# A two-layer encoder trunk with its residual stream turned: features on partitions instead of tokens, and the RMS taken by a product with ones

## The chip, the cores and the metric

One core of a Trainium2 chip runs the whole program in one launch. The metric is the device time of that launch in microseconds. Three runs of the kernel before were timed, and one more execution was taken with the hardware profiler.

## What is computed

There are 512 tokens of 1024 features, and two layers. Each layer is a mixer with a gate, a residual add, and a gated per-layer embedding (PLE). The reference, cut to what matters here:

```python
def rmsnorm(x, g):
    y = x * rsqrt(mean(x * x, axis=-1) + EPS)
    return y * g

for i in range(2):
    xn = rmsnorm(x, norm_g[i])
    if i == 0:                      # neighbourhood attention, 16 heads of 64
        q, k, v, z = split(xn @ na_w_in)
        y = (na(q, k, v, rpb) * silu(z)) @ na_w_out
    else:                           # latent attention, 16 heads
        c_q, c_kv, k_rope, z = split(xn @ mla_w_in)
        y = (mla(c_q, c_kv, k_rope) * silu(z)) @ mla_w_out
    h = x + y
    gate = sigmoid(rmsnorm(h, ple_norm[i]) @ ple_w_gate[i])
    x = h + gate * (p[i] @ ple_w_proj[i])
return rmsnorm(x, final_norm)
```

All matrices are float32.

## The kernel before

**Products.** Each operand is split into a high and a low part of the matmul type fp32r, and a product is three matmuls for each 128 rows of its contraction: high by high, low by high, high by low. A tile over 1024 features is 24 matmuls of 128 x 128 by 128 x 512. `load_w` (L67 to L78) brings weights: a DMA into `wraw`, a copy to `whi` on ACT (L76), and the rest `wlo = wraw - whi` on POOL (L77). Weight buffers rotate: three in the common pool, and more in a pool of the stage (`extra=True`).

**Layouts.** The attention parts already work with features on partitions: their input `xT` is the normalised x with 128 features on the partitions and 512 tokens along the row, split into `xh` and `xl`. The residual stream is the other way: four tiles of 128 tokens by 1024 features (`x`, later `r`). So every normalisation is in rows. `rms` (L100 to L107) squares a tile on ACT with a sum along the row, takes (mean + eps) to the power -0.5 of that one column on POOL (L106), and multiplies on DVE by it and by the gain (L107). After it `rows_to_cols` turns the tile with eight TensorE transposes (L118), and `split` makes the high and low parts (L83 on ACT, L85 on DVE). This is done for x (tiles named `xn`), for h in both layers (`hn`), and for the x between the layers (`x1n`).

**Stages, in order.**

- Start: x is loaded, normalised and turned; PLE's product p @ w_proj (`ple`) runs on TensorE meanwhile and is written to DRAM.
- `z_phase` makes five of the eight gate tiles of layer 0; then the 16 heads, and the last three gate tiles.
- `out_proj` (L345): for each half n of the 1024 output features and each of four token tiles t, 24 matmuls with the attention output as stationary operand and the weights (512 columns) moving. A tile is added to `r` (L357). When n is 1, tile t is complete, and `norm_h` normalises and turns it into `hnT[t]`.
- `gate_phase` (L383): the same loops over n and t with `hnT[t]` stationary; sigmoid on ACT (L398), times the PLE tile (L399), added to `r` (L401). In layer 0 a complete tile is stored to `spill`, normalised and turned into `x1T`. In layer 1 `done` scales each tile with the final norm and sends it out (L636 to L649); the last tile is cut into two halves of 256 columns.
- Layer 1: `mla_c` makes the compressed q and kv and the rotary key with tokens on partitions (`c`), normalises them there and turns them (`cn`); then seven gate tiles, the heads, PLE of layer 1 and again `out_proj` and `gate_phase`.

**Order.** The order on each engine is made when the program is built: a scheduler that simulates a timeline places each instruction, and every engine then runs its own list strictly in that order, each instruction waiting for what it needs. PSUM tiles rotate by tag: two for `mm`, two for `S`, three for `T`, one for `O`.

Of the kernel before, what the change touches and what calls it, by code (L numbers as in the profile page):

```python
# [19 lines left out]
P = 128  # L20
S = 512
# [17 lines left out]
class Trunk:  # L39
    def __init__(self, tc, ctx, a, dbg=None):  # L40
# [10 lines left out]
        self.half = self.const.tile([P, 1], F32, name="half")  # L51
        nc.vector.memset(self.half, -0.5)
# [3 lines left out]
        self.spill = [dram.tile([P, D], F32, name=f"spill{t}") for t in range(NT)]  # L56
        self.pe = [[dram.tile([P, D], F32, name=f"pe{l}{t}") for t in range(NT)] for l in range(2)]
# [50 lines left out]

    def bcast(self, pool, ap, n, name, tag=None, bufs=None):
# [11 lines left out]
    def rows_to_cols(self, xn, dst):  # L121

        for g in range(2):
            t = self.transposes([xn[:, (4 * g + i) * P:(4 * g + i + 1) * P] for i in range(4)])
            hi, lo = dst(g)
            self.split(hi, lo, t.rearrange("p (a b) -> p a b", a=4))


    def proj_T(self, out, w, xT):
        whi, wlo = w  # L130
        xh, xl = xT
        t = []
        W = lambda a, k: a[:, k * P:(k + 1) * P]
        X = lambda a, k: a[k // 4][:, k % 4, :]
        t += [(W(whi, k), X(xh, k)) for k in range(KD)]
        t += [(W(whi, k), X(xl, k)) for k in range(KD)]
        t += [(W(wlo, k), X(xh, k)) for k in range(KD)]
        return self.mms(out, t)

    def z_phase(self, wap, xT, js, after=None):  # L140
        zs = {}
        for j in js:
            w = self.load_w(wap[j], 1024)
            ps = self.psum("mm")
            self.proj_T(ps, w, xT)
            z = self.zp.tile([P, S], F32, name="z", tag="z")
            with self.tc.issue_after(after) if after is not None else nullcontext():
                self.nc.scalar.activation(z, ps, AF.Silu)  # L148
            zs[j] = z
        return zs  # L150
# [194 lines left out]
    def out_proj(self, wap, oT, res, after, last_mm):  # L345
        nc = self.nc
        for n in range(2):
            ws = [self.load_w(wap[n, c], 1024, extra=n == 1 or c == 3) for c in range(4)]
            for t in range(NT):
                ps = self.psum("S" if n == 0 and t >= 2 else "mm")  # L350
                L = lambda s, k: oT[s][k // 4][:, k % 4, t * P:(t + 1) * P]
                W = lambda s, k: ws[k // 2][s][:, (k % 2) * S:(k % 2 + 1) * S]
                m = self.by_chunk(L, W)
                with self.tc.issue_after(last_mm):
                    self.mms(ps, m)
                r = res[t][:, n * S:(n + 1) * S]
                nc.vector.tensor_tensor(out=r, in0=ps, in1=r, op=ALU.add)  # L357
                if n == 1:
                    after(t)
# [7 lines left out]
    def ple(self, pool, layer, tag, bufs, operands):  # L367
        nc, a = self.nc, self.a
        pT, wj = operands
        for n in range(2):  # L370
            if n == 1:
                wj = self.load_w(a["proj"][layer, n], 1024)
            for t in range(NT):
                pp = self.psum("mm")
                L = lambda s, k: pT[s][:, k * S + t * P:k * S + (t + 1) * P]
                W = lambda s, k: wj[s][:, k * S:(k + 1) * S]
                self.mms(pp, [(L(s, k), W(r, k)) for k in range(2) for s, r in ((0, 0), (1, 0), (0, 1))])
                o = pool.tile([P, S], F32, name="pe", tag=tag, bufs=bufs)
                nc.scalar.copy(o, pp)
                nc.sync.dma_start(self.pe[layer][t][:, n * S:(n + 1) * S], o)  # L380


    def gate_phase(self, pool, layer, hnT, res, after):  # L383
        nc, a = self.nc, self.a
        for n in range(2):
            ws = [self.load_w(a["gate"][layer, n, c], 1024, extra=n == 1 or c == 3) for c in range(4)]
            for t in range(NT):
                pe = pool.tile([P, S], F32, name="pe", tag="pe", bufs=3)
                nc.sync.dma_start(pe, self.pe[layer][t][:, n * S:(n + 1) * S])
                last = layer == 1 and n == 1 and t == NT - 1  # L390
                w = S // 2 if last else S
                for o in range(0, S, w):
                    ps = self.psum("mm")[:, :w]
                    L = lambda s, k: hnT[t][:, s * KD + k, :]
                    W = lambda s, k: ws[k // 2][s][:, (k % 2) * S + o:(k % 2) * S + o + w]
                    self.mms(ps, self.by_chunk(L, W))
                    sg = pool.tile([P, S], F32, name="sg", tag="sg", bufs=2)[:, :w]
                    nc.scalar.activation(sg, ps, AF.Sigmoid)  # L398
                    nc.vector.tensor_tensor(out=sg, in0=pe[:, o:o + w], in1=sg, op=ALU.mult)  # L399
                    r = res[t][:, n * S + o:n * S + o + w]  # L400
                    nc.vector.tensor_tensor(out=r, in0=r, in1=sg, op=ALU.add)  # L401
                    after(t, n, o, w)


    def mla_c(self, pool, xT, cT, sets):
# [5 lines left out]
        cs = [pool.tile([P, 672], F32, name=f"c{t}", tag="c", bufs=4) for t in range(NT)]  # L411
        xh, xl = xT
        L = lambda s, k, t: s[k // 4][:, k % 4, t * P:(t + 1) * P]
        for part, (w0, wn) in enumerate(((0, 384), (384, 288))):
            ws = [self.load_w(a["mla_c"][part][c], 2 * wn, extra=c == 3) for c in range(4)]
            for t in range(NT):
# [3 lines left out]
                nc.scalar.activation(cs[t][:, w0:w0 + wn], ps[:, :wn], AF.Copy)  # L420
# [31 lines left out]
    def mla_heads(self, pool, xT, cT, sets, oT):  # L452
# [79 lines left out]
        zs = self.z_phase(a["mla_z"], xT, range(NEARLY))  # L532
        group(0)
        last = project(0)
        zs.update(self.z_phase(a["mla_z"], xT, range(NEARLY, 8)))
# [33 lines left out]
    def run(self):  # L569
        tc, nc, a = self.tc, self.nc, self.a  # L570
        xT = ([self.bigtile(f"xh{g}") for g in range(2)], [self.bigtile(f"xl{g}") for g in range(2)])

        def colsT(xT, t):
            return lambda g: (xT[0][g][:, :, t * P:(t + 1) * P], xT[1][g][:, :, t * P:(t + 1) * P])

        with tc.tile_pool(name="pre", bufs=4, reuse_waits="tile") as pool:
            operands = self.ple_load(0)
            nc.sync.dma_start(self.ident, a["ident"])
            xt = []
            for t in range(NT):  # L580
                x = pool.tile([P, D], F32, name="x", tag="x")
                nc.sync.dma_start(x, a["x"][t])
                xt.append(x)
                if t == 0:
                    g0 = self.bcast(pool, a["norm_g"][0], D, "g0")
            for t in range(NT):
                xn = pool.tile([P, D], F32, name="xn", tag="xn", bufs=4)
                self.rms(xn, xt[t], g0, D)
# [172 lines left out]
```

## Time and profile before

| | |
|---|---|
| three timed runs, median | 693.58 us (693.12 to 693.97) |
| the profiled execution, whole | 693.59 us |
| its span in the trace | 691.8 us |
| mean granted TensorE clock | 0.998 |
| TensorE matmul busy | 665.2 us, 3580 matmuls |
| TensorE weight load busy | 566.7 us |
| DVE busy | 353.1 us |
| ACT busy | 400.9 us |
| POOL busy | 398.1 us |

The page of a profile gives, for one execution, the busy time of each engine, then the span in 40 equal slices with a digit for each engine (tenths of the slice in which it was busy), then the chain of waits that ended last, and groups of equal instructions with their count, busy time and mean duration. "L96 PE" is what line 96 of the kernel issued on TensorE (the helper `mms` records most matmuls, so tiles are told apart by name: `ps_mm<-whi,hnT` is a gate tile). DVE is VectorE, ACT ScalarE, POOL GpSimd, SP the engine that issues the DMAs. The ends of matmuls are modelled, so their starts are what one measures by.

### The profile page before, as it was taken

What the parts mean: (1) busy time and instruction counts of PE and PEld (TensorE: products, weight loads), DVE (VectorE), ACT (ScalarE), POOL (GpSimd) and SP (SyncE); (2) the same over time, 40 slices, a digit from 0 to 9 for tenths busy, and PEclk for the clock granted to TensorE, in tenths of its full rate; (3) what the DMA queues carried; (4) which work ended last, traced back from release to release, by engine and by line L of the source; (5) the groups of instructions that cost most, each with busy time, mean ns of one, the idle gap of its engine ahead of it and who ended that gap; (6) DMA issues with size and microseconds to landing.
All of it is one profiled execution on the core that took longest, in us unless ns stands there. A gap on an engine that the chain in (4) does not pass through costs nothing.

```text
span 691.8 us, 10087 instructions
## 1 busy us (share of the span) xinstructions
PE 665.2 (96%) x3580; PEld 566.7 (82%) x3580; DVE 353.1 (51%) x805; ACT 400.9 (58%) x799; POOL 398.1 (58%) x309
## 2 busy tenths in 40 slices
PE   5999999999999999999999998999999999999995
PEld 4789898998988888878899886787888777887885
DVE  4300364637837611573624503688988886015633
ACT  6722576666767562543443634878888877416423
POOL 1753557466575566933044634777789766659411
PEclk9999999999999999999999999999999999999999
DMA  8731423323223127433242344213121202575122
GB/s 320 238 118 62 137 81 104 104 73 107 73 92 116 42 105 292 165 118 131 86 116 92 115 112 124 81 24 92 25 70 39 84 1 77 188 300 183 31 74 93
DMA packets 28642, 77.53 MB, mean 112 GB/s; under 512 B 3632, under 2 KB 6704, under 8 KB 28592
## 3 DMA queue, kind: packets, MB, share of 16 engines
q1 hardware_dynamic: 28592, 76.89, 33.4%
q8 instruction: 28, 0.46, 0.3%
q14 instruction: 22, 0.18, 0.1%
HBM read 65.34 MB, written 8.39 MB: 107 GB/s over the span
## 4 chain that ended last, share of the span: by engine, by line
PE 82%; ACT 6%; DVE 4%; POOL 3%; issue 2%; DMA 2%; SPq 0%; POOLq 0%; DVEq 0%; ACTq 0%
PE ps_mm L96 60%; PE ps_S L96 8%; PE ps_T L118 4%; PE ps_O L96 4%; POOL wlo L77 3%; PE ps_O L331 2%; PE ps_T L319 1%; ACT whi L76 1%; ACT ex L558 1%; DMA x<-x 1%; PE ps_S L284 1%; PE ps_S L283 1%; DVE mx L556 1%; DVE hn L107 0%; DMA wraw<-mla_c 0%
## 5 line engine op out<-in xcount | busy, mean ns | idle before, releaser
L77 POOL TENSOR_TENSOR wlo<-wraw,whi 128x1024 fp32r<-128x1024 f32 (+3 forms) x96 | 218.7, 2290 | 118.0 <-ACT whi L76 68.1
L76 ACT ACTIVATE whi<-wraw 128x1024 fp32r<-128x1024 f32 (+4 forms) x100 | 98.0, 988 | 105.8 <-PE ps_mm L96 38.7
L560 POOL TENSOR_TENSOR ex<-ex,rc 128x512 f32<-128x512 f32 x64 | 66.2, 1047 | 20.7 <-DVE rc L559 14.0
L96 PE MATMUL ps_mm<-whi,hnT 128*128 128x512 f32 (+1 forms) x272 | 71.2, 380 | 0.6 <-ACT hnT L83 0.6
L96 PEld LDWEIGHTS ps_mm<-whi,hnT 128*128 128x128 f32 x272 | 48.9, 188 | 9.9 <-ACT hnT L83 1.0
L306 POOL TENSOR_TENSOR ex<-ex,rc 128x128 f32<-128x128 f32 (+1 forms) x64 | 34.3, 560 | 38.2 <-DVE rc L302 36.6
L556 DVE TENSOR_REDUCE mx<-ps_S 128x1 f32<-128x512 f32 x64 | 43.7, 685 | 15.3 <-PE ps_S L96 14.3
L96 PE MATMUL ps_mm<-xh,whi 128*128 128x512 f32 x192 | 50.9, 398 | 0.1
L96 PE MATMUL ps_mm<-xh,wlo 128*128 128x512 f32 x192 | 49.1, 391 | 0.0
L558 ACT ACTIVATE ex<-ps_S,mx 128x512 f32<-128x512 f32 x64 | 44.0, 689 | 8.2 <-DVE mx L556 6.7
L96 PE MATMUL ps_mm<-xl,whi 128*128 128x512 f32 x192 | 48.6, 392 | 0.0
L85 DVE TENSOR_TENSOR pt_lo<-ps_T,pt_hi 128x512 fp32r<-128x512 f32 x64 | 43.1, 679 | 5.0 <-ACT pt_hi L83 4.6
L106 POOL TENSOR_TENSOR rs<-ss,half 128x1 f32<-128x1 f32 x24 | 14.1, 591 | 50.8 <-DVE ss L105 50.8
L301 ACT ACTIVATE ex<-ex,mx 128x128 f32<-128x128 f32 (+1 forms) x64 | 30.2, 473 | 22.0 <-DVE mx L297 21.6
L96 PEld LDWEIGHTS ps_mm<-xl,whi 128*128 128x128 f32 x192 | 35.6, 188 | 7.3
L96 PEld LDWEIGHTS ps_mm<-xh,wlo 128*128 128x128 f32 x192 | 35.6, 188 | 7.1
L83 ACT ACTIVATE pt_hi<-ps_T 128x512 fp32r<-128x512 f32 x64 | 37.0, 598 | 7.5 <-PE ps_T L118 7.3
L96 PE MATMUL ps_mm<-wlo,hnT 128*128 128x512 f32 (+1 forms) x136 | 40.6, 379 | 0.0
L96 PEld LDWEIGHTS ps_mm<-xh,whi 128*128 128x128 f32 x192 | 34.4, 188 | 6.5 <-ACT z L148 0.4
L118 PE MATMUL ps_T<-ident,ex 128*128 128x128 f32 x256 | 36.3, 273 | 0.2 <-DVE pt_lo L85 0.2
L118 PEld LDWEIGHTS ps_T<-ident,ex 128*128 128x128 f32 x256 | 30.7, 140 | 6.8 <-issue 0.7
L85 DVE TENSOR_TENSOR vt<-ps_mm,vt 128x256 fp32r<-128x256 f32 x32 | 13.2, 415 | 44.3 <-ACT vt L83 44.0
(215 smaller groups left out, 1573.0 us busy)
## 6 DMA issues: line engine op xcount, KB each, us to landing
pe<-pe SPq DMA_DIRECT2D x32, 256.0 KB, 2.9
wraw<-na_qk SPq DMA_DIRECT2D x16, 512.0 KB, 3.3
wraw<-gate SPq DMA_DIRECT2D x16, 512.0 KB, 3.3
wraw<-na_z SPq DMA_DIRECT2D x8, 512.0 KB, 3.8
wraw<-na_v SPq DMA_DIRECT2D x8, 512.0 KB, 3.3
wraw<-na_o SPq DMA_DIRECT2D x8, 512.0 KB, 3.3
wraw<-mla_z SPq DMA_DIRECT2D x8, 512.0 KB, 3.9
wraw<-mla_o SPq DMA_DIRECT2D x8, 512.0 KB, 3.4
```

Of the source, the lines that this page charges most:

```text
L76: nc.scalar.activation(hi[:, c], raw[:, c], AF.Copy)
L77: (rest or nc.gpsimd).tensor_tensor(out=lo[:, c], in0=raw[:, c], in1=hi[:, c].bitcast(F32), op=ALU.subtract)
L83: nc.scalar.activation(hi, src, AF.Copy, scale=scale)
L85: nc.vector.tensor_tensor(out=lo, in0=src, in1=hi.bitcast(F32), op=ALU.subtract)
L96: last = nc.tensor.matmul(out, l, r, start=i == 0, stop=i == n - 1)
L106: nc.gpsimd.tensor_tensor(out=rs, in0=ss, in1=self.half, op=ALU.pow)
L118: self.nc.tensor.transpose(t[:, i * P:(i + 1) * P], b, self.ident)
L301: self.last_exp = nc.scalar.activation(e, e, AF.Exp, bias=mx[:, qt:qt + 1], accum_out=sm[:, qt:qt + 1])
L306: nc.gpsimd.tensor_tensor(out=e, in0=e, in1=rc[:, qt:qt + 1].to_broadcast([P, e.shape[1]]), op=ALU.mult)
L556: nc.vector.reduce_max(mx[:, c], sp, axis=AX.X, negate=True)
L558: nc.scalar.activation(ex, sp, AF.Exp, bias=mx[:, c], accum_out=sm[:, c])
L560: nc.gpsimd.tensor_tensor(out=ex, in0=ex, in1=rc[:, c].to_broadcast([P, S]), op=ALU.mult)
```

## The change

The residual stream is kept with features on partitions from beginning to end: x comes in turned (`xT` in DRAM, eight tiles of 128 features by 512 tokens), `res` is one tile of eight such blocks, and the output leaves the same way.

- The output projection, PLE's product and the gates are computed as eight tiles j of 128 features by 512 tokens, the weights stationary and the activations moving, as z already was.
- No tile of x, h or x1 is transposed. The transposes of the softmax rows and of `cn` remain.
- The sum of squares over features runs over partitions: `add_square` squares each tile on ACT and adds it to `acc` on POOL (DVE for the first stage and for the last tile of others); `col_rms` splits `acc` in two, multiplies it by a 128 x 128 matrix of ones on TensorE (two matmuls, so each partition holds the sum of each token), adds eps on DVE, and takes the power -0.5 of 128 x 512 numbers on POOL.
- At the start the root `R` and the gain scale x before it is split. In the other places the split takes h or x1 times the gain, without the root, and the products' results are multiplied by the root when they leave PSUM: `Rh` in the gates, `r1` in layer 1's z, and `r1c` (the same numbers as a column, by four small DMAs) in `mla_c`. Final norm: `R2`, multiplied into the output.
- Two of layer 1's gate tiles are computed ahead of `mla_c`, five after it. In the gate stage of layer 1 the last three tiles are cut into 384 and 128 columns.
- Weight buffers: the first two output weights come from the common pool, the other six and all eight gate weights rotate through the stage's five.

The diff, cut to its core:

```diff
+    def add_square(self, pool, acc, src, first, fast=False):
+        nc = self.nc
+        if first:
+            nc.scalar.activation(acc, src, AF.Square)
+            return
+        sq = pool.tile([P, S], F32, name="sq", tag="sq", bufs=2)
+        sq = sq[:, :src.shape[1]]
+        nc.scalar.activation(sq, src, AF.Square)
+        (nc.vector if fast else nc.gpsimd).tensor_tensor(out=acc, in0=acc, in1=sq, op=ALU.add)
+
+    def col_rms(self, pool, R, acc):
+        nc = self.nc
+        n = acc.shape[1]
+        ah = pool.tile([P, S], F32R, name="ah", tag="ah", bufs=1)[:, :n]
+        al = pool.tile([P, S], F32R, name="al", tag="al", bufs=1)[:, :n]
+        nc.scalar.activation(ah, acc, AF.Copy)
+        nc.vector.tensor_tensor(out=al, in0=acc, in1=ah.bitcast(F32), op=ALU.subtract)
+        ps = self.psum("S")[:, :n]
+        self.mms(ps, [(self.ones, ah), (self.ones, al)])
+        nc.vector.tensor_scalar(R, ps, D * EPS, None, op0=ALU.add)
+        nc.gpsimd.tensor_tensor(out=R, in0=R, in1=self.half.to_broadcast([P, n]), op=ALU.pow)
...
-    def z_phase(self, wap, xT, js, after=None):
+    def z_phase(self, wap, xT, js, after=None, parts=None, R=None):
...
+                    nc.vector.tensor_tensor(out=z, in0=ps, in1=R, op=ALU.mult)
+                    nc.scalar.activation(z, z, AF.Silu, scale=32.0)
...
     def out_proj(self, wap, oT, res, after, last_mm):
+        def finish(j, ps):
+            nc.vector.tensor_tensor(out=res[:, j, :], in0=ps, in1=res[:, j, :], op=ALU.add)
+            after(j)
+        ws = [self.load_w(wap[j], 1024) for j in range(2)]
+        pss = [self.psum("mm") for j in range(2)]
+        with self.tc.issue_after(last_mm):
+            self.proj_T2(pss, ws, self.by_k(oT))
...
+        for j in range(2, KD):
+            w = self.load_w(wap[j], 1024, extra=True)
+            ps = self.psum("mm")
+            self.proj_T(ps, w, oT)
+            finish(j, ps)
...
+    def gate_phase(self, pool, layer, hT, Rh, res, after, blocks):
+        def load(j):
+            w = self.load_w(a["gate"][layer, j], 1024, extra=True)
+            pe = pool.tile([P, S], F32, name="pe", tag="pe", bufs=3)
+            nc.sync.dma_start(pe, self.pe[layer][j])
+            return w, pe
+        def tile_(j, w, pe, c):
+            n = c.stop - c.start
+            ps = self.psum("mm")[:, :n]
...
+            nc.vector.tensor_tensor(out=sg, in0=ps, in1=Rh[:, c], op=ALU.mult)
+            nc.scalar.activation(sg, sg, AF.Sigmoid, scale=32.0)
+            nc.vector.tensor_tensor(out=sg, in0=pe[:, c], in1=sg, op=ALU.mult)
+            r = res[:, j, c]
+            nc.vector.tensor_tensor(out=r, in0=r, in1=sg, op=ALU.add)
+            after(j, c)
...
     def mla_c(self, pool, xT, cT, sets):
+        for t in range(NT):
+            nc.sync.dma_start(r1c[:, t:t + 1], self.r1[0:1, t * P:(t + 1) * P])
+        nc.vector.tensor_scalar(r1c, r1c, 32.0, None, op0=ALU.mult)
...
-                nc.scalar.activation(cs[t][:, w0:w0 + wn], ps[:, :wn], AF.Copy)
+                nc.scalar.activation(cs[t][:, w0:w0 + wn], ps[:, :wn], AF.Copy, scale=r1c[:, t:t + 1])
...
     def run(self):
+            for k in range(KD):
+                x = pool.tile([P, S], F32, name="x", tag="x", bufs=8)
+                nc.sync.dma_start(x, a["xT"][k])
+                xs.append(x)
+                self.add_square(pool, acc, x, k == 0, True)
+            R = pool.tile([P, S], F32, name="R", bufs=1)
+            self.col_rms(pool, R, acc)
+            for k in range(KD):
+                x = xs[k]
+                hi, lo = (xT[s][k // 4][:, k % 4, :] for s in range(2))
+                nc.vector.scalar_tensor_tensor(x, x, self.gain(0, k, True), R, op0=ALU.mult, op1=ALU.mult)
+                nc.scalar.activation(hi, x, AF.Copy)
+                nc.gpsimd.tensor_tensor(out=lo, in0=x, in1=hi.bitcast(F32), op=ALU.subtract)
...
+                def turned(T, j, gi):
+                    hi, lo = (T[s][j // 4][:, j % 4, :] for s in range(2))
+                    r, g = res[:, j, :], self.gain(gi, j)
+                    nc.scalar.activation(hi, r, AF.Copy, scale=g)
+                    nc.vector.scalar_tensor_tensor(lo, r, g, hi.bitcast(F32), op0=ALU.mult, op1=ALU.subtract)
+                def done_h(j):
+                    turned(hT, j, 2 + layer)
+                    self.add_square(pool, acc, res[:, j, :], j == 0, j == KD - 1)
+                self.out_proj(a["na_o"] if layer == 0 else a["mla_o"], oT, res, done_h, last)
+                self.col_rms(pool, Rh, acc)
...
+                        self.col_rms(pool, R2[:, c], acc2[:, c])
+                        for i in range(0, KD, 2):
+                            o = res[:, i:i + 2, c]
...
+                            (nc.gpsimd if i == 6 else nc.vector).tensor_tensor(out=o, in0=o, in1=b, op=ALU.mult)
+                            nc.sync.dma_start(a["out"][i:i + 2, :, c].rearrange("j p t -> p j t"), o)
+                    blocks = lambda j: [slice(0, S)] if j < 5 else [slice(0, 384), slice(384, S)]
+                self.gate_phase(pool, layer, hT, Rh, res, done, blocks)
+                if layer == 0:
+                    self.r1 = self.zp.tile([P, S], F32, name="r1", tag="z")
+                    self.col_rms(pool, self.r1, acc2)
...
+                zs = self.z_phase(a["mla_z"], x1T, range(2), parts=self.by_k(x1T), R=self.r1)
```

More of the change, by code (lines that the diff above doesn't have):

```diff
@@ L145, in z_phase @@
             self.proj_T(ps, w, xT)
[L146 to L149, printed above, removed]
+            finish(j, ps)
         return zs
@@ L369, in ple @@
         pT, wj = operands
[L370 to L380, printed above, removed]
@@ L383, in gate_phase @@
-    def gate_phase(self, pool, layer, hnT, res, after):
-        nc, a = self.nc, self.a
[L385 to L402, printed above, removed]
@@ L577, in run @@
             operands = self.ple_load(0)
+            nc.sync.dma_start(self.gains[:, :40], a["gains"])
+            nc.vector.tensor_scalar(self.gains[:, 40:], self.gains[:, :40], 32.0, None, op0=ALU.mult)
             nc.sync.dma_start(self.ident, a["ident"])
[L579 to L585, printed above, removed]
```

213 lines of the change are left out of this document (117 added, 96 removed).

## The prediction

> **What bounds the kernel now.** I read the page first (busy times, slices, chain of waits), then the chain in order of time, then TensorE's own waits.
>
> ```profile
> span 691.8 us, 10087 instructions
> ...
> PE 665.2 (96%) x3580; PEld 566.7 (82%) x3580; DVE 353.1 (51%) x805; ACT 400.9 (58%) x799; POOL 398.1 (58%) x309
> ...
> PE   5999999999999999999999998999999999999995
> ...
> PEclk9999999999999999999999999999999999999999
> ...
> PE 82%; ACT 6%; DVE 4%; POOL 3%; issue 2%; DMA 2%; SPq 0%; POOLq 0%; DVEq 0%; ACTq 0%
> ```
>
> ```profile
> 24.39 57.84 PE ps_mm L96 x300
> ...
> 83.18 5.47 PE ps_mm L96 x24
> ```
>
> ```profile
> PE ps_mm L96 <- ACT whi L76: 6.3, 1, 6.3
> ...
> PE ps_T L118 <- DVE hn L107: 1.5, 1, 1.5
> ...
> PE ps_mm L96 <- ACT c L420: 0.7, 1, 0.7
> ...
> PE ps_mm L96 <- DVE r L357: 0.7, 2, 0.3
> PE ps_mm L96 <- ACT hnT L83: 0.6, 1, 0.6
> ```
>
> TensorE is the bound from first to last slice, at the full granted clock. Matmuls of 512 columns follow each other every 5.47/24 = 0.228 us, whichever operand is stationary, so swapping activations and weights costs nothing by itself. Every other engine is near half busy. So two things decide: how many TensorE slots go or come, and every microsecond in which TensorE now has to wait. The four waits after the start above (hn, c, r, hnT: 3.5 us) belong to the layer ends that the change rewrites.
>
> The profiled execution took 693.59 us (span 691.8, the rest around it); the median of the three runs is 693.58, so one sum serves for both. About 0.2% is what a measurement of this kernel can tell from no change.
>
> **TensorE's slots.**
>
> ```profile
> 333.76 1.03 PE L118 MATMUL ps_T<-ident,x1n 128*128 128x128 f32 x8
> 334.56 0.71 PE L96 MATMUL ps_mm<-whi,hnT 128*128 128x512 f32 x2
> 335.10 0.62 PE L96 MATMUL ps_mm<-wlo,hnT 128*128 128x512 f32 x2
> ...
> 341.91 0.51 PE L96 MATMUL ps_mm<-whi,x1h 128*128 128x384 f32 x2
> 342.25 0.52 PE L96 MATMUL ps_mm<-whi,x1l 128*128 128x384 f32 x2
> ```
>
> ```profile
> L118 PE MATMUL ps_T<-ident,hn 128*128 128x128 f32 x64 | 8.7, 273 | 1.5 <-DVE hn L107 1.5
> L118 PE MATMUL ps_T<-ident,xn 128*128 128x128 f32 x32 | 4.6, 279 | 2.7 <-DVE xl L85 1.5 <-DVE xn L107 1.1
> ...
> L118 PE MATMUL ps_T<-ident,x1n 128*128 128x128 f32 x32 | 4.1, 272 | 0.0
> ```
>
> Eight transposes take 334.56 - 333.76 = 0.80 us, and the two matmuls after them 0.54 instead of 0.46: 0.88/8 = 0.11 us each. The 96 transposes of hn and x1n go: 96 x 0.11 = 10.5 us off the path (the 32 of xn lie in the start, below). In come the products with ones: two of 512 columns for Rh and r1 in layer 0 (0.9 us together), two for Rh in layer 1 and two of 384 columns for R2 (0.8). The last three gate tiles are cut into 384 and 128 columns: 24 matmuls at 0.17 (341.91 to 342.25 for two) and 24 at some 0.10 (the transposes are 128 wide too), 6.5 instead of 5.5 us, so +3.2 for three. PLE and output projections keep their counts. The four waits go too (-3.5): the first gate tile now runs chunk by chunk over unnormalised h, and eighteen of its matmuls (4.1 us) lie over the last tile's add, copy and subtraction. Slots and old waits: -10.5 + 0.9 + 0.8 + 3.2 - 3.5 = -9.1 us.
>
> **The new step: a power over 512 columns.** Four times the whole row of 512 reciprocal roots is computed on all 128 partitions by one POOL instruction (R, Rh, r1, Rh again), and once more in two pieces (R2). Before, POOL did it for one column. Call the price of 512 columns X.
>
> ```profile
> L77 POOL TENSOR_TENSOR wlo<-wraw,whi 128x1024 fp32r<-128x1024 f32 x80 | 194.4, 2442 | 80.9 <-ACT whi L76 46.0 <-PE ps_mm L96 29.0 <-ACT ph L83 2.9
> L560 POOL TENSOR_TENSOR ex<-ex,rc 128x512 f32<-128x512 f32 x64 | 66.2, 1047 | 20.7 <-DVE rc L559 14.0 <-PE ps_S L96 2.9 <-PE ps_T L118 2.8
> ...
> L164 POOL TENSOR_TENSOR u<-u,z 128x512 f32<-128x512 f32 x16 | 20.6, 1291 | 19.6 <-DVE u L159 18.8 <-ACT z L148 0.5
> L77 POOL TENSOR_TENSOR wlo<-wraw,whi 128x768 fp32r<-128x768 f32 x8 | 14.7, 1847 | 23.6 <-ACT whi L76 20.5 <-issue 3.1
> L106 POOL TENSOR_TENSOR rs<-ss,half 128x1 f32<-128x1 f32 x24 | 14.1, 591 | 50.8 <-DVE ss L105 50.8
> ...
> L306 POOL TENSOR_TENSOR ex<-ex,rc 128x128 f32<-128x128 f32 x16 | 6.4, 400 | 28.4 <-DVE rc L302 26.8 <-DVE mx L297 1.5
> ...
> L643 POOL TENSOR_TENSOR rs<-mn,half 128x1 f32<-128x1 f32 x4 | 2.2, 548 | 15.9 <-DVE mn L637 15.9
> ```
>
> A product with a broadcast column costs 400 ns for 128 columns and 1047 for 512: 1.68 ns a column on top of 185. One column of power costs 548, so 361 ns of power beyond a product's fixed part. Low end: 512 columns cost what a product of that size costs, 1.29 us. Scaled by fixed parts (548/185), 1.68 ns becomes 5.0 and X = 3.1 us: the columns overlap as well as a product's do. High end: they do not overlap at all, 0.19 + 512 x 0.361 = 185 us. Nothing in between is shown. The geometric middle of 1.29 and 185 is 15; I take X = 10 us (20 ns a column, a pass overlapped eighteen times), a little nearer the products, since everything else on this engine overlaps its columns. It is a choice, and it carries the forecast.
>
> ```profile
> L76 ACT ACTIVATE whi<-wraw 128x1024 fp32r<-128x1024 f32 x80 | 83.9, 1058 | 87.3 <-PE ps_mm L96 27.0 <-issue 17.6 <-DMA wraw<-mla_o 16.3
> ...
> L107 DVE SCALAR_TENSOR_TENSOR xn<-x,rs,g 128x1024 f32<-128x1024 f32 x4 | 5.1, 1281 | 1.3 <-POOL rs L106 1.3
> ...
> L401 DVE TENSOR_TENSOR r<-r,sg 128x512 f32<-128x512 f32 x15 | 10.4, 692 | 0.5
> ...
> L398 ACT ACTIVATE sg<-ps_mm 128x512 f32<-128x512 f32 x15 | 9.0, 598 | 27.9 <-PE ps_mm L96 27.9
> ...
> L399 DVE TENSOR_TENSOR sg<-pe,sg 128x256 f32<-128x256 f32 x2 | 0.9, 426 | 0.6 <-ACT sg L398 0.6
> ```
>
> **Where X is on the path.** *Start.* R stands before the split of x, so nothing of the gates z can begin without it; PLE's 48 matmuls (10.9 us) are the only cover.
>
> ```profile
> 6.32 0.80 PE L96 MATMUL ps_mm<-whi 128*128 128x512 f32 x1 [6.32 <-ACT whi L76]
> ...
> 9.05 0.47 PE L96 MATMUL ps_mm<-whi,wlo 128*128 128x512 f32 x1
> ```
>
> ```profile
> 37.89 0.61 PE L96 MATMUL ps_mm<-xh,whi 128*128 128x512 f32 x2
> ```
>
> ```profile
> L582 SPq DMA_DIRECT2D x<-x x4: 432/520/1069, 3.1 to 5.1; - x4
> ...
> DMA to landing us min/median/max: 5.4/7.9/8.9
> ```
>
> Before, two tiles of z are done at 37.9. The last x lands at 5.1 + 8.9 = 14.0; the change drops the gain broadcast queued between them, so some 12.5. Then on ACT a square, a PLE copy, the split of PLE's second weights and the copy of acc (0.6 + 0.6 + 1.06 + 0.6: 15.4), on DVE the subtraction 0.7, the ones, the add of epsilon 0.7: 17.2. POOL, in order, stands behind two weight splits (2 x 2.44 after 14.8) and starts the power at 19.7. Behind it on POOL wait two more splits and eight subtractions for xl: 4.9 + 8 x 1.29 = 15.2; the last two matmuls end 0.5 later. Two tiles of z are done at 35.4 + X: X - 2.5 against before.
>
> *Rh, twice.* Both PSUM buffers of the gate stage hold tiles that need Rh to be emptied, so TensorE has two tiles and two products with ones as cover: 50 x 0.228 = 11.3 us from the end of the output projection. In the built order the power stands on POOL behind the split of the sixth gate weight, whose buffer (five rotate) comes free when the first gate tile is done, 33 matmuls or 7.5 us in; plus 1.06 on ACT and 2.44 on POOL is 11.0. Then X, and DVE's 0.7 that empties the buffer, with handovers 0.8. Each wait is X + 0.5: the cover is used up before the power begins.
>
> *r1.* Two z tiles, the ones and 44 matmuls of 384 columns cover 10.9 + 0.45 + 7.5 = 18.9 us. The power stands behind two splits of 1.85 that begin at some 11.1: 14.8 + X + 0.7. (They begin there because their buffers come free as the two z tiles end.) Wait X - 3.5 if positive. On SP the four small transfers that turn r1 into a column, r1c, wait for it too, and behind them stand the last two weight chunks of the c projection; those are wanted two tiles of 384 columns (8.2 us) and more after r1 is there, so I put nothing on that; late, they would cost what they lack of it.
>
> *At nothing* I put the squares, their sums, the gain copies and the extra product with Rh or r1. A tile is 5.5 us of TensorE. Over a gate tile ACT has 1.06 + 3 x 0.6 = 2.9, DVE 4 x 0.69 = 2.8, POOL 2.44 + 1.29 = 3.7. POOL is the closest to the edge; were it late by a whole sum, 1.3 us a layer would appear.
>
> *End.*
>
> ```profile
> 684.49 0.38 ACT L398 ACTIVATE sg<-ps_mm 128x256 f32<-128x256 f32 x1 [0.28 <-PE ps_mm L96]
> ...
> 688.47 0.38 SPq L648 DMA_DIRECT2D out<-r  x1
> ```
>
> Before, 7.3 us pass from the last PSUM tile (684.49) to the span's end, 3.3 of them after the last issue. Now: eight steps on 128 columns at about 0.3 (0.426 for 256), ones and epsilon 0.6, then on DVE three products of 768 columns (1.28 x 3/4 = 0.95) and three of 256 (0.43), two more issues 0.7, landing 3.3: 11.3, so +4.0 whatever X below 5. Above, the two powers set it: X + 0.4, POOL's own products 1.85 + 0.7, issue and landing 3.7: X + 6.6, so X - 0.7, taken as X - 1.
>
> *Clock.* The six matmuls from 6.32 to 9.05 came 0.45 us apart instead of 0.228: TensorE had idled 6.3 us, and paid 1.4. I put 1.4 on each of the three waits where X is 4 or more: +4.2. The Trainium skill (TensorE: Matmul & The Clock Gate, "What's actually happening") says that the clock is halved after an idle window of some 3.4 us and freed after a busy one; the trace agrees at the start, and has no such gap later to show it.
>
> Sum: -9.1 (slots) - 2.5 (start) + 1.0 (Rh) = -10.6 without X, plus 3X, plus (X - 3.5), plus the end. X = 10: -10.6 + 30 + 6.5 + 9.0 + 4.2 = +39: 733 us.
>
> **Rivals.** *The power is as cheap as a product.* X = 1.29: -10.6 + 3.9 + 4.0 = -2.7: 690.9 us, faster. For it: every other row of POOL. Against it: 548 against 185 ns for a single column. It decides below X = 2.2, where the sum is zero (X = 3.1 gives 696). Chance 0.27, and 0.04 for X about 2.2.
>
> *The power overlaps only a few passes.* Eight passes in flight: 361/8 = 45 ns a column, X = 23.3: -10.6 + 69.9 + 19.8 + 22.3 + 4.2 = +106: 799 us. For it: 361 ns for one column is a long chain. With no overlap it would be near 1,600. Against it: nothing in the trace. Chance 0.27, of which 0.12 for over 850 (X over 33). The Trainium skill (GPSIMD Engine Reference, 7, Performance pitfalls) has 4 cycles for each dependent fp32 step and two slots that can issue them: at most eight steps in flight, which is this rival; no run here shows it.
>
> *The forecast*, X from 2.5 to 16, 694.5 to 763 us, chance 0.42, likeliest 733.
>
> The range reaches from 688 (the cheap power, with 3 us for the constants) to 850: some 0.08 is left out below and 0.12 above. Faster 0.27, same 0.04, slower 0.69.
>
> **What would show it.** POOL's power rows of 512 columns give X at once: under 2 us and the forecast is wrong in size and sign. TensorE's waits should show the second multiplication of PSUM by Rh as releaser twice, X + 0.5 each; the first matmul on xh should start at some 21 + X; 128 matmul slots on ident should be gone, and the last PSUM tile lie 11 us or more before the end. If the waits at Rh are short though X is large, the order on POOL was read wrongly; if X is small and the time still rises, the end or the cut tiles were undersized.

## The result: 1120 us, and the profile after

| | before | changed |
|---|---|---|
| timed runs, median | 693.35 us (691.74 to 693.97, 4 runs) | 1120.24 us (1119.5 to 1120.46, 4 runs) |
| ratio, 95% interval | | 1.616 (1.613 to 1.618) |
| span of the profiled execution | 691.8 us | 1118.6 us |
| mean granted TensorE clock | 0.998 | 0.806 |

The prediction was 733 us, range 688 to 850: slower, as forecast, and far outside the range. The page of the changed kernel:

```profile
span 1118.6 us, 10053 instructions
...
PE 673.6 (60%) x3512; PEld 572.3 (51%) x3512; DVE 389.6 (35%) x822; ACT 415.0 (37%) x807; POOL 841.7 (75%) x327
...
PE   5001999999989910099002996999999940068000
...
POOL 4999745566666799964997643778867879963998
PEclk9555999999999965599555998999999975579555
...
PE 51%; POOL 37%; DVE 4%; ACT 4%; issue 2%; DMA 1%; SPq 1%; DVEq 0%; POOLq 0%; ACTq 0%
```

TensorE does nearly the same work (674 us busy, was 665) in a span 427 us longer. Its row has five holes, and POOL is busy in all of them. TensorE's waits name what ends four of them (engine and line that waits, what it waited for: total, times, longest):

```profile
PE ps_mm L98 <- DVE sg L459: 163.9, 2, 81.9
PE ps_mm L173 <- ACT xh L670: 83.5, 6, 80.5
PE ps_mm L98 <- DVE z L190: 77.6, 1, 77.6
PE ps_mm L98 <- DVE vt L87: 8.9, 1, 8.9
...
PE ps_O L386 <- DVE u L214: 4.1, 1, 4.1
```

DVE's `sg` is the multiplication by `Rh`, its `z` that by `r1`, and `xh` is made from x times `R`; `vt` (V tiles) and `u` (attention output) are waits of another kind, that come back below. Behind the first three stands one line. The groups, shapes kept apart (busy, mean ns of one):

```profile
L138 POOL TENSOR_TENSOR Rh<-Rh,half 128x512 f32<-128x512 f32 x2 | 163.9, 81948 | 0.0
L138 POOL TENSOR_TENSOR r<-r,half 128x512 f32<-128x512 f32 x1 | 81.9, 81925 | 0.0
L138 POOL TENSOR_TENSOR R<-R,half 128x512 f32<-128x512 f32 x1 | 81.9, 81915 | 0.0
L138 POOL TENSOR_TENSOR R<-R,half 128x384 f32<-128x384 f32 x1 | 61.5, 61537 | 0.7 <-DVE R L137 0.7
L138 POOL TENSOR_TENSOR R<-R,half 128x128 f32<-128x128 f32 x1 | 20.7, 20717 | 0.0
...
L108 POOL TENSOR_TENSOR rs<-ss,half 128x1 f32<-128x1 f32 x8 | 4.2, 543 | 16.7 <-DVE ss L107 16.7
```

So X = 81.9 us, where the forecast had 10. The three widths lie on a line: (81.9 - 20.7) / 384 = 159.4 ns for each further column, and 0.3 us beside it.

### The profile page after: what moved, and what is told of

It reads as the page before. It is cut to its first block, busy times and chain, and to the rows that moved or that the text cites. A ratio compares the mean times of both kernels' runs of the same rounds, so it can differ in the third digit from the quotient of the medians.

```text
span 1118.6 us, 10053 instructions
## 1 busy us (share of the span) xinstructions
PE 673.6 (60%) x3512; PEld 572.3 (51%) x3512; DVE 389.6 (35%) x822; ACT 415.0 (37%) x807; POOL 841.7 (75%) x327
## 4 chain that ended last, share of the span: by engine, by line
PE 51%; POOL 37%; DVE 4%; ACT 4%; issue 2%; DMA 1%; SPq 1%; DVEq 0%; POOLq 0%; ACTq 0%
PE ps_mm L98 37%; POOL R L138 15%; POOL Rh L138 15%; POOL r L138 7%; PE ps_mm L173 3%; PE ps_S L98 3%; PE ps_O L98 2%; PE ps_T L149 2%; DVE x L669 1%; PE ps_O L386 1%; ACT ex L635 1%; DMA wraw<-proj 1%; PE ps_T L374 1%; ACT pt_hi L85 1%; SPq L92 1%
## 5 line engine op out<-in xcount | busy, mean ns | idle before, releaser
L138 POOL TENSOR_TENSOR R<-R,half 128x512 f32<-128x512 f32 (+2 forms) x3 | 164.1, 54723 | 0.7 <-DVE R L137 0.7
L138 POOL TENSOR_TENSOR Rh<-Rh,half 128x512 f32<-128x512 f32 x2 | 163.9, 81948 | 0.0
L98 PE MATMUL ps_mm<-hh,whi 128*128 128x512 f32 (+2 forms) x152 | 37.8, 387 | 163.9 <-DVE sg L459 163.9
L98 PEld LDWEIGHTS ps_mm<-hh,whi 128*128 128x128 f32 x152 | 28.6, 203 | 169.6 <-DVE sg L459 164.7
L138 POOL TENSOR_TENSOR r<-r,half 128x512 f32<-128x512 f32 x1 | 81.9, 81925 | 0.0
L460 ACT ACTIVATE sg<-sg 128x512 f32<-128x512 f32 (+2 forms) x19 | 10.6, 563 | 172.5 <-DVE sg L459 172.5
L459 DVE TENSOR_TENSOR sg<-ps_mm,Rh 128x512 f32<-128x512 f32 (+2 forms) x19 | 11.3, 604 | 179.0 <-POOL Rh L138 165.0
L125 POOL TENSOR_TENSOR acc<-acc,sq 128x512 f32<-128x512 f32 (+2 forms) x27 | 35.9, 1330 | 45.9 <-ACT sq L124 45.9
L98 PE MATMUL ps_mm<-whi,x1h 128*128 128x288 f32 (+1 forms) x48 | 12.5, 337 | 77.6 <-DVE z L190 77.6
L173 PEld LDWEIGHTS ps_mm<-xh,whi 128*128 128x128 f32 x16 | 3.7, 233 | 87.1 <-ACT xh L670 86.4
```

The lines of the kernel that those rows point to most:

```text
L98: last = nc.tensor.matmul(out, l, r, start=i == 0, stop=i == n - 1)
L125: (nc.vector if fast else nc.gpsimd).tensor_tensor(out=acc, in0=acc, in1=sq, op=ALU.add)
L138: nc.gpsimd.tensor_tensor(out=R, in0=R, in1=self.half.to_broadcast([P, n]), op=ALU.pow)
L173: self.nc.tensor.matmul(out, l, r, start=n[o] == 0, stop=n[o] == 23)
```

## The experiments

"Product" below is the changed kernel with POOL's power replaced by a POOL product of the same shape; it leaves the root out, so it shows times and not the result wanted, and so do the f runs, h1_all and p1_part32. All runs were timed in rounds with the kernel before, whose medians were 693.45 to 693.72 us. Its single runs spread over 691.7 to 695.3, more than the 0.2% that the prediction reckoned with, so differences of a microsecond or two between medians say little.

| run | median, us | ratio to before (95%) |
|---|---|---|
| e1_product | 717.25 | 1.035 (1.033 to 1.037) |
| e2_sqrt | 735.91 | 1.061 (1.059 to 1.063) |
| e2_lnexp | 733.50 | 1.058 (1.056 to 1.060) |
| e3_cols | 752.56 | 1.085 (1.083 to 1.087) |
| f1_fill | 716.88 | 1.033 (1.030 to 1.036) |
| f2_rope | 712.11 | 1.027 (1.024 to 1.029) |
| f3_end | 714.06 | 1.030 (1.027 to 1.032) |
| f4_start | 714.97 | 1.031 (1.028 to 1.034) |
| h1_all | 700.17 | 1.009 (1.006 to 1.011) |
| h2_lnall | 715.49 | 1.032 (1.029 to 1.034) |
| h3_lnwide | 710.87 | 1.024 (1.022 to 1.027) |
| p1_part32 | 1135.88 | 1.638 (1.633 to 1.642) |

**The power taken out (e1_product).**

```diff
-        nc.gpsimd.tensor_tensor(out=R, in0=R, in1=self.half.to_broadcast([P, n]), op=ALU.pow)
+        nc.gpsimd.tensor_tensor(out=R, in0=R, in1=self.third.to_broadcast([P, n]), op=ALU.mult)
```

> The power in the root over the columns is replaced by a POOL product of the same shape with a small constant column (the reciprocal root is left out: the numbers that come out are not the reference's). Theory (the price of the power, five times on the path, is the whole loss): X falls from 81.9 to about 1.3 us and the prediction's own sum holds, 690.9 us (686 to 696), with no TensorE wait above 5 us after the start. Rival (the change carries costs of its own that the sum put at nothing: the sum with X = 81.9 gives 1092, the measured 1120 is 28 more, of which 9.2 us is a stall in front of the MLA heads and 4.4 us one near the end of the NA heads): these stay, and the time is 700 to 715 us.

717.25 us, far above the theory's 691 and just above the rival's 700 to 715. The power is 403 of the 427 us, and costs of the change itself are the rest: with a root at the price of a product the change is still 3.5% slower. TensorE's waits of this run:

```profile
PE ps_mm L100 <- DVE vt L89: 8.7, 1, 8.7
PE ps_mm L100 <- ACT whi L80: 7.3, 2, 6.4
PE ps_S L100 <- ACT ah L135: 6.6, 1, 6.6
PE ps_O L388 <- DVE u L216: 4.1, 1, 4.1
PE ps_S L100 <- ACT ex L637: 3.6, 4, 1.8
PE ps_mm L100 <- DVE sg L461: 3.0, 3, 1.0
```

The 163.9 at the gates is 3.0 here, and the 80.5 at the start is gone. (`whi`, 6.4, is the first weight's arrival, as before.) The starts of matmuls in the two profiled executions (before 693.59 us, product 715.60) show where the remaining 22 us come in (x1 is the stream between the layers, cT the turned latent):

| up to | before | product | late by |
|---|---|---|---|
| third tile of z | 37.9 | 41.6 | +3.7 |
| first gate tile, layer 0 | 292.6 | 301.2 | +8.6 |
| first product with x1 | 341.9 | 347.7 | +5.8 |
| first product with cT | 415.2 | 418.7 | +3.5 |
| first gate tile, layer 1 | 637.8 | 650.2 | +12.4 |
| last gate matmul | 684.2 | 699.9 | +15.8 |
| end of span | 691.8 | 713.7 | +21.9 |

**The root elsewhere (e2_sqrt, e2_lnexp).**

```diff
-        nc.gpsimd.tensor_tensor(out=R, in0=R, in1=self.half.to_broadcast([P, n]), op=ALU.pow)
+        nc.scalar.activation(R, R, AF.Sqrt)          # e2_sqrt
+        nc.vector.reciprocal(R, R)
+        nc.scalar.activation(R, R, AF.Ln)            # e2_lnexp
+        nc.scalar.activation(R, R, AF.Exp, scale=-0.5)
```

> The same root, computed by ACT's Sqrt and DVE's reciprocal over 512 columns instead of POOL's power. Theory: what counts is the duration of the root, whoever computes it: 0.6 on ACT, a reload of ACT's tables before and after it (1.28 us each in the trace) and some 0.7 on DVE make X about 2.6 to 3.9, and the time 3 to 8 us above the run with the product. Rival (the power's place on POOL, behind weight splits, costs more than its duration): up to 3 us below the run with the product.

> The same root by two ACT passes, exp(-0.5 ln s). Theory: two ACT passes of 0.6 us and up to three table loads of 1.28: X of 2.5 to 5, within 5 us of the run with Sqrt. Rival (table loads fall into ACT's queue in front of the weight casts and hold the gate weights up, which the sum has at nothing): 10 us or more above the run with the product.

Both compute the whole thing, and both are 16 to 19 us above the product, far more than the 3 to 8 that the theory of e2_sqrt had. The groups of e2_sqrt:

```profile
L138 ACT ACT_TABLE_LOAD x6 | 7.7, 1283 | 0.1
L139 DVE RECIPROCAL Rh<-Rh 128x512 f32<-128x512 f32 x2 | 6.7, 3353 | 5.1 <-ACT Rh L138 5.1
```

A reciprocal of 512 columns takes DVE 3.35 us, not the 0.7 of a product. With load, root and reciprocal (1.28 + 0.6 + 3.35) X is some 5.2, and the two waits at `Rh` are 10.8 us together. The prediction's sum puts 17.8 us between X = 1.29 and X = 5.2; measured are 18.7. In e2_lnexp there are two table loads for each root; the waits are 7.9. Its time is within 5 us of e2_sqrt and more than 10 above the product, as its theory and its rival had it, but the rival's reason doesn't show: at the gates of both traces TensorE waits for `sg`, that is for the root, and never for a weight.

**The power on four columns (e3_cols).**

```diff
+        for t in range(nt):     # sums as a column per token tile
+            self.mms(pt[:, 2 * t:2 * t + 2], [(ah[:, b], self.ones[:, 0:2]), (al[:, b], self.ones[:, 0:2])])
+        nc.gpsimd.tensor_tensor(out=r4, in0=r4, in1=self.half.to_broadcast([P, nt]), op=ALU.pow)
+        for t in range(nt):     # diagonal tiles, split in two, then ones x diagonal gives the rows again
+            nc.vector.tensor_scalar(dg[:, t * P:(t + 1) * P], self.ident, r4[:, t:t + 1], None, op0=ALU.mult)
```

> The sums of squares are taken as a column per token tile (four pairs of products of the squares with two columns of ones), POOL's power runs over 4 columns instead of 512, and the result is spread over the partitions again through four diagonal tiles and two products with ones. Theory (POOL's power costs 159 ns for each column, whatever else): the power takes 0.3 + 4 x 0.159 = about 1.0 us; with the steps around it (0.3 + 1.0 + 4 x 0.25 + 0.6 + 0.7 + 0.5 + 0.6) the whole detour is 5 to 7 us, the sum gives 705 to 715 us. Rival (a power has a large fixed price that the 512 columns share): the power takes many microseconds even here and the time is above 730.

```profile
L143 POOL TENSOR_TENSOR r<-r,half 128x4 f32<-128x4 f32 x4 | 4.1, 1024 | 0.0
```

The power is as expected (1.02 us, 80 times less than for the same numbers held on every partition), so its price is one per column. The last one, for the two blocks of the final norm, has three columns and one:

```profile
734.96 0.87 POOL L143 TENSOR_TENSOR r<-r,half 128x3 f32<-128x3 f32 x1 [0.53 <-DVE r L141]
...
743.31 0.55 POOL L143 TENSOR_TENSOR r<-r,half 128x1 f32<-128x1 f32 x1 [1.83 <-DVE r L141]
```

0.55, 0.87 and 1.02 us for one, three and four columns: some 159 ns for each further one here too, and 0.39 us beside them. The time, 752.6, is not as expected, and though it lies where the rival had it, the power is not the cause. TensorE waits 18.9 us in five places for the split of the diagonals alone:

```profile
PE ps_S L98 <- ACT ah L147: 18.9, 5, 5.5
```

At `Rh` of layer 0 it takes 9.5 us from the first column product to `Rh` (319.10 to 328.56), where 5 to 7 were expected for the whole detour; one of the four diagonal tiles took DVE 2.37 us instead of 0.28.

**Partitions (p1_part32).**

```diff
+        nc.gpsimd.tensor_tensor(out=junk, in0=R[0:32], in1=self.half[0:32].to_broadcast([32, n]), op=ALU.pow)
         nc.gpsimd.tensor_tensor(out=R, in0=R, in1=self.third.to_broadcast([P, n]), op=ALU.mult)
```

> The kernel with the product (the root left out), with a power of the same columns on 32 partitions instead of 128 put ahead of each product on POOL, its result unused. Theory (the price is 159 ns for each column of a partition, and partitions run side by side): 81.9 us a power again, 1120 us. Rival (the price is by element): 20.5 us a power, about 717 + 5 x 20 = 815 us.

```profile
L141 POOL TENSOR_TENSOR sq<-Rh,half 32x512 f32<-32x512 f32 x2 | 163.9, 81933 | 0.0
...
L141 POOL TENSOR_TENSOR sq<-R,half 32x384 f32<-32x384 f32 x1 | 61.5, 61527 | 8.4 <-DVE R L139 8.4
L141 POOL TENSOR_TENSOR sq<-R,half 32x128 f32<-32x128 f32 x1 | 20.7, 20717 | 4.5 <-DVE R L139 4.5
```

A quarter of the partitions costs the same 81.9 us: 159 ns is for a column, whether 32 or 128 partitions take part. The run, 1135.9 us, is 16 above the theory's 1120: the products that stand behind the powers take 5.4 us in all, and three of them start 2.3 to 4.6 us after their power.

**The 24 us that are left with a cheap root: four covers, one at a time.** Each edit is made on the product kernel.

```diff
-        pss = [self.psum("mm") for j in range(2)]      # f1_fill, in out_proj
+        pss = [self.psum("S") for j in range(2)]
```

> On the kernel with the product in place of the power (the root left out), the first two tiles of the output projection take PSUM buffers of S instead of mm, as half of the first four did in the kernel before. Theory (the changed projection takes mm buffers, which the last tiles of z still hold, so nothing can fill the end of the NA heads: a stall of 4.4 us and some 1.2 us at a lowered clock after it): the stall goes, 5 us less, 712. Rival (the stall comes from VectorE being late there, whatever the buffers): no change, 717.

The stall at `u` is gone, as the theory had it, and from the third tile of z to the first gate tile TensorE needs 256.7 us, not 259.7. But a wait of 2.5 for `oh` comes in its place, and the same edit made layer 1's way to its gates 2.7 us longer: 716.9, nothing in all.

```diff
+                for t, n in zip(self.rope, ("rope_c", "rope_s")):    # f2_rope: ahead of mla_c, not in mla_heads
+                    nc.sync.dma_start(t, a[n])
```

> On the kernel with the product (the root left out), the two rotation tables are loaded ahead of the c projection instead of behind it. Theory (taking two z tiles ahead of the c projection leaves five behind it to cover the chain over the latent, its twelve moves and, last in SP's queue, the tables; the DVE multiplication that waits for them holds up the emptying of PSUM: a stall of 9.0 us and some 2 us of lowered clock): the stall falls to 2 us or less, 707 to 710. Rival (the twelve moves themselves are late, the tables only land with them): at most 2 us less, 715.

5.1 us less: 712.1, between what theory and rival named. In the product kernel SP issues the table at 427.80, behind the latent's twelve moves; it lands 4.6 us later, DVE's `xr` waits for it, and DVE's `vt`, next in its list, holds TensorE's PSUM:

```profile
427.80 0.42 SPq L535 DMA_DIRECT2D rope_c<-rope_c  x1
...
432.39 0.69 DVE L561 TENSOR_TENSOR xr<-xr,rope_c 128x512 f32<-128x512 f32 x1 [8.63 <-DMA rope_c<-rope_c]
433.00 0.75 DVE L89 TENSOR_TENSOR vt<-ps_mm,vt 128x256 fp32r<-128x256 f32 x2
...
433.47 2.93 PE L100 MATMUL ps_mm<-cT,whi 128*128 128x512 f32 x6 [8.68 <-DVE vt L89]
```

With the tables early, theory and rival turn out to be both there: 5.1 us of the wait stay, since `vt` lies in memory that the moves still read:

```profile
430.96 0.66 ACT L87 ACTIVATE vt<-ps_mm 128x256 fp32r<-128x256 f32 x2 [6.04 <-DMA qo<-slab_l]
```

```diff
-                    blocks = lambda j: [slice(0, S)] if j < 5 else [slice(0, 384), slice(384, S)]    # f3_end
+                    blocks = lambda j: [slice(0, S)] if j < 5 else [slice(0, 256), slice(256, S)]
-                            (nc.gpsimd if i == 6 else nc.vector).tensor_tensor(out=o, in0=o, in1=b, op=ALU.mult)
+                            (nc.gpsimd if i >= 4 else nc.vector).tensor_tensor(out=o, in0=o, in1=b, op=ALU.mult)
```

> On the kernel with the product (the root left out), the last three gate tiles are cut 256/256 instead of 384/128 and POOL takes two of the four last products instead of one. Theory (128 columns cost TensorE 1 us a tile more, and VectorE runs three products of 768 columns, 4.3 us, ahead of the last tile's own steps): 3 us less from the cut, 2 to 3 from the order, 711 to 712. Rival (the last block's chain of ten steps sets the end and grows with its columns): within 1 us of 717.

3.2 us less, half of what was expected, and by the traces all of it from the new widths: from the first gate tile of layer 1 to the last gate matmul it is 46.4 us, 49.7 in the product kernel. From there to the end it is 15.0 us, 13.8 in the product kernel. There, three products of the first block stand ahead of the last tile's addition on DVE, which could have begun near 701.2:

```profile
700.90 0.29 DVE L463 TENSOR_TENSOR sg<-pe,sg 128x128 f32<-128x128 f32 x1 [0.38 <-ACT sg L462]
...
701.11 4.29 DVE L732 TENSOR_TENSOR res<-res,R 128x768 f32<-128x768 f32 x3
...
705.33 0.28 DVE L465 TENSOR_TENSOR res<-res,sg 128x128 f32<-128x128 f32 x1
```

In f3_end that addition comes 1.9 us sooner after the last gate matmul (3.5 against 5.4), but with 256 columns the steps behind it take 3.0 us more (11.4 against 8.4), which is the rival. The edit made both changes at once; what the order alone is worth was not run.

```diff
-                nc.gpsimd.tensor_tensor(out=lo, in0=x, in1=hi.bitcast(F32), op=ALU.subtract)    # f4_start
+                nc.vector.tensor_tensor(out=lo, in0=x, in1=hi.bitcast(F32), op=ALU.subtract)
```

> On the kernel with the product (the root left out), the eight subtractions for xl run on DVE instead of POOL. Theory (in the start POOL does two weight splits and then eight subtractions that end at 40.4 us, and DVE's eight multiplications take 1.46 instead of 0.69 us beside it: this is the 4.9 us by which the start came out later than the sum had it): the third tile of z starts near 37 instead of 41.6 us, 4 to 5 us less, 712 to 713. Rival (DVE becomes the bound of the start instead): no change within 1.5 us.

2.3 us less, about the spread of single runs, and in the trace the third tile of z comes no sooner: 42.25, and 41.55 in the product kernel. The two executions differ in the clock. In f4_start 18 matmuls come 0.427 instead of 0.228 us apart in the stretch before that tile (18.84 to 21.83 and 30.86 to 35.55), in the product kernel's execution none: by an estimate from these gaps, 3.6 us. h1_all below has the same edit and no such matmuls in that stretch, and its third tile of z comes at 38.79, 2.8 us before the product kernel's.

**All of them together (h1_all, h2_lnall, h3_lnwide).** f2, f3 and f4 as above, f1 in layer 0 alone, and the slab moved away from `vt`; h3 also gives gate tiles 2 and 3 other PSUM buffers:

```diff
-        slab_h = pool.tile([P, S], F32R, name="slab_h", tag="slab", bufs=2)
-        slab_l = pool.tile([P, S], F32R, name="slab_l", tag="slab", bufs=2)
+        slab = self.bigtile("slab")
+        slab_h, slab_l = slab[:, 0, :], slab[:, 1, :]
-            ps = self.psum("mm")[:, :n]                               # h3_lnwide
+            ps = self.psum("S" if j in (2, 3) else "mm")[:, :n]
```

> The kernel with the product (the root left out) with all edits at once: early projection tiles on S buffers in layer 0 alone, rotation tables loaded early, the latent's slab in a buffer that the V tiles do not take over (so that they no longer wait for the twelve moves), gate tiles cut 256/256 with two of four last products on POOL, xl on DVE. Theory (the 24 us that the changed kernel loses even with a free root are these four separate covers): 3.0 (layer-0 stage of the fill) + 5.1 + 5 (slab) + 3.2 + 2.3 = 18.6 us less than 717.3: 697 to 701, near the 690.9 that the prediction had for a root at the price of a product. Rival (each removed wait is replaced by the next one): above 706.

> The same edits with the whole computation, the root as exp(-0.5 ln s) on ACT. Theory: 733.5 - 18.6 = 715. Rival: above 722.

> As the run before, and gate tiles 2 and 3 take PSUM buffers of S, so that four tiles (22 us) instead of two cover the root. Theory (the waits at Rh are the root's latency beyond a cover of 11 us, 4.5 to 7 us each with the lowered clock): they go, 8 to 12 us less, 703 to 707. Rival (weights for the third and fourth tile are not there in time): within 3 us of the run before. To beat the kernel before it would have to come below 692.

h1_all: 700.2, 17.1 us below the product where 18.6 was expected; the covers nearly add up. Its waits, against those of the product kernel:

```profile
PE ps_mm L100 <- ACT whi L80: 7.0, 2, 6.1
PE ps_S L100 <- ACT ah L135: 5.7, 1, 5.7
PE ps_S L100 <- ACT ex L634: 3.6, 4, 1.8
PE ps_mm L100 <- DVE sg L461: 2.9, 3, 1.0
PE ps_S L175 <- ACT oh L224: 2.5, 1, 2.5
...
PE ps_mm L100 <- DVE vt L89: 0.8, 1, 0.8
```

`vt` fell from 8.7 to 0.8 and `u` is gone. h2_lnall, with the whole computation, is 715.5, as expected (715), but partly by luck. From the first product with cT to layer 1's gates it is 15.3 us shorter than e2_lnexp (220.6 against 235.9), more than the 10.7 that h1_all gained there on the product kernel, and its start got worse: the third tile of z comes at 46.0, and at 42.8 in e2_lnexp. TensorE waits 5.0 us for the low part of a weight (`wlo`), a wait that neither e2_lnexp nor h1_all has. Two weight splits on POOL last 9.88 us together, where two alone take 4.9, while DVE does f4's eight subtractions one behind the other:

```profile
27.77 9.88 POOL L79 TENSOR_TENSOR wlo<-wraw,whi 128x1024 fp32r<-128x1024 f32 x2 [6.54 <-ACT whi L78]
...
28.23 4.90 DVE L669 TENSOR_TENSOR xl<-x,xh 128x512 fp32r<-128x512 f32 x8
```

h3_lnwide is 4.6 lower, half of what was hoped: layer 1's wait at `Rh` goes, but 4.0 us for one tile in layer 0 stays, and so does the wait for `wlo` (4.3). At 710.9 it is the best of the kernels that compute everything, and 2.4% slower than before. No run points to a version that beats the kernel before.

## Why the prediction was wrong, and where it was right

**The step that failed: the price X.** "The geometric middle of 1.29 and 185 is 15; I take X = 10 us (20 ns a column, a pass overlapped eighteen times), a little nearer the products". Measured: 81.9 us. The prediction took a product's fixed part (0.19 us) for the power's, so it read 361 ns of power into the one-column row; e3_cols shows that row to be 0.39 us fixed and 159 ns a column. Its choice of 10 us then meant an overlap of eighteen, drawn towards the products. No run shows passes that overlap: every further column, from the second to the 512th, cost 159 ns. Since X stands five times in the sum, 71.9 us too little are 359.5 us. The range went wrong at the same step: its upper end stood for X of 33, and the rival above stopped at eight passes in flight, with nothing in the trace to say so. The Trainium skill (GPSIMD Engine Reference, "7. Performance pitfalls for Q7 kernels") has 4 cycles a step for a dependent fp32 chain and a twofold co-issue. Eight in flight was the prediction's own estimate from these two, and at 45 ns a column it was 3.5 times too cheap.

**The second step: what was put at nothing.** With X = 1.29 the sum gave 690.9; the product kernel took 717.3, so the constants were 26.4 too low. 359.5 + 26.4 = 386 of the 387 us between forecast and result. The rival of a cheap power would have been wrong in sign too. The constants, by step:

- *Counts of matmuls stood for stages.* The two z tiles were costed as moved work without price. Moved ahead of `mla_c`, they no longer cover the latent's moves and the tables in SP's queue. In the kernel before SP issued the twelve moves from 404.56, 10.7 us ahead of the first product with cT (415.21); in the product kernel from 419.02, 0.3 us behind it (418.69). The 11 us between are two tiles. It cost 8.7 us of wait, and matmuls at 0.427 instead of 0.228 us for a while after. From the first product with cT to the next output projection h1_all is 10.7 us shorter than the product kernel (176.8 against 187.5): f2's edit and the slab.
- *"PLE and output projections keep their counts"* overlooked which PSUM buffers they use. `S` tiles let the projection begin under the last heads (f1: the stall of 4.1 goes, 3.0 us up to the gates, and layer 1 loses it again).
- *Start.* X - 2.5 was forecast, for X = 1.29 a gain of 1.2; the product kernel lost 3.7. Part of it is POOL and DVE side by side (below); with f4's edit h1_all is 2.8 us earlier there.
- *End.* 11.3 us from the last tile forecast, 13.8 in the product kernel. The sum had the three products of 768 columns at 2.9 us and they took 4.3; the steps on 128 columns and the sum with ones took 4.2 instead of 3.0.

**Right.** *Places.* Each of the five waits came where the sum had it, and the form of the sum held: from X = 1.29 to 81.9 it gives 401 us with the clock's 4.2, measured 403. *Rh:* X + 0.5 was forecast; the gaps between matmuls in the changed kernel are 394.75 to 477.07 and 907.21 to 989.54, 82.1 beyond a matmul's own time: X + 0.2. The power begins as the cover ends, behind the sixth gate weight's split (on POOL from 391.98; the power starts at 394.35):

```profile
20.71 81.92 POOL R L138
...
393.10 2.05 PE ps_mm L98 x9
395.18 81.12 POOL Rh L138
477.07 34.66 PE ps_mm L98 x144
...
525.60 81.94 POOL r L138
608.30 11.05 PE ps_mm L98 x48
```

*r1:* X - 3.5 = 78.4, measured 77.6. *End:* X + 6.6 = 88.5 from the last tile, measured 90.5 (1028.1 to 1118.6). *Start:* the first matmul on `xh` was put at 21 + X = 102.9 and came at 106.2, the two tiles of z 7.1 us later than 35.4 + X. *Clock:* 1.4 us for each wait; the first matmuls after the waits at 477.07, 608.30 and 989.54 come at 0.427 us (0.320 for 384 columns, later 0.173) and cost some 1.7, 2.5 and 1.5 more. By stage (PE, PEld, DVE, ACT, POOL busy, then the granted clock):

```profile
394.75:477.07 82.32, 0.39 (x2) 0.00 (x1) 0.74 (x2) 2.36 (x3) 82.32 (x2) 0.52 0.02 6
477.07:490.00 12.93, 12.93 (x50) 10.57 (x51) 10.64 (x10) 6.85 (x10) 9.29 (x5) 0.87 0.51 156
```

The mean of 0.806 is thus mostly a result of the waits: the clock is granted low while TensorE has nothing to do. The squares, their sums and the four transfers for `r1c` cost nothing that a wait shows.

## What to carry to other kernels

Holding a row statistic on all 128 partitions multiplies the elementwise work on it by 128 (512 columns here instead of four of one): price it by that very operation, not by its neighbours on the engine. One length alone can't tell a fixed price from a price per column; time a second length, or let the range reach to no overlap. Count what a moved or re-laid stage was covering (PSUM buffers, transfers behind it in a queue, the next stage's memory), not only its instructions. A sum of waits whose places are right stays usable when one price turns out wrong.

## What the runs showed of the hardware

A power on POOL took 159 ns a column and 0.3 to 0.4 us beside them, 81.9 us for 512 columns, the same on 32 partitions as on 128; a product of that shape took 1.0 to 1.3 us. DVE's reciprocal took 3.35 us for 512 columns.

DVE and POOL slow each other. The eight multiplications of x in the start, in the product kernel (ns: least, median, most), where POOL is busy beside them:

```profile
L671 DVE SCALAR_TENSOR_TENSOR x<-x,gains,R x8: 744/1252/2885, 21.2 to 30.1; 128x512 f32<-128x512 f32 x8
```

and in f4_start, where POOL is idle from 21.4 to 26.65 and busy with two weight splits up to 33.0, the same line, and the subtractions that run on DVE there:

```profile
L671 DVE SCALAR_TENSOR_TENSOR x<-x,gains,R x8: 746/747/754, 21.4 to 26.0; 128x512 f32<-128x512 f32 x8
...
L673 DVE TENSOR_TENSOR xl<-x,xh x8: 679/684/2853, 26.7 to 35.3; 128x512 fp32r<-128x512 f32 x8
```

Two of those, beside the splits, took 2.20 and 2.85 us instead of 0.68, so 1.5 and 2.2 more, each less than one split (2.4). POOL is held up as well: the two splits took 3.56 and 2.81 us here, and 9.88 together in h2_lnall, 5.0 more than alone, beside subtractions that lasted 4.9. The Trainium skill (SBUF — State Buffer, "SBUF: two separate sides") describes such a lock: a DVE operation with two inputs in SBUF and a GpSimd instruction that reads SBUF exclude each other, and whichever starts first has the shared ports for its whole length. The traces agree.
